# Inverse roots of eighteen norms: spread over the partitions through a line in DRAM instead of by matmuls

## The chip, the cores and the metric

The kernel runs on one core of a Trainium2 chip. The core has a matmul engine (PE, with its weight loads shown apart as PEld), three engines for elementwise work (DVE, ACT and POOL), a queue SP that issues most transfers, and 16 DMA engines. Each engine takes its own instructions in order and waits on semaphores for what others make. The metric is the device time of one execution in microseconds (us); lower is better.

## The reference

One decoder block on x of 2048 tokens with 1024 features, all in fp32:

```python
def rmsnorm(x, g):
    r = lax.rsqrt(jnp.mean(xf * xf, axis=-1, keepdims=True) + EPS)
    return xf * r * g

hn = rmsnorm(h, norm1_g)
proj = jnp.einsum('bsd,de->bse', hn, w_in)           # u_pool | q | k | v
y_pool = pool_mixer(u_pool, pool_w, pool_scale)
o = stick_breaking_attention(q, k, v)                 # 8 heads of 64
mixed = concatenate([rmsnorm(y_pool, pool_out_g), rmsnorm(o, attn_out_g)])
h = h + mixed @ w_out
hn2 = rmsnorm(h, norm2_g)
h = h + square(relu(hn2 @ w_up)) @ w_down             # 4096 wide
return rmsnorm(h, final_g)
```

Every `rmsnorm` needs, for each token, the inverse root `r` of the mean of the squares over its features.

## The kernel before

Activations lie transposed: features over the 128 partitions (P), tokens along the row. The 2048 tokens are four tiles j of T = 512 (NT = 4); 1024 features are KD = 8 chunks of 128. A tile of 512 tokens is TB = 4 blocks of 128.

A product in fp32 precision is made of three matmuls in fp32r: each operand is cut into a high and a low half by `split` (a copy on ACT, line 146, then a subtraction on DVE, line 147), and high by high, high by low and low by high are added (lines 178 to 180, 1102, 1275 and 1452). PE's stream is thus a long row of these matmuls: input projection, the attention of earlier tiles between them, output projection, and an FFN that takes two pairs of tiles and forms seven products in place of eight (`up` with PSUM tiles pX, pY, pZ; `down` with pb). Work beside the projections is put into a list `later` and let out a few pieces for each weight tile, so each engine's order is that in which the pieces are written, with the norms' root part set ahead by `tc.high_priority()`, and with `gates` that hold some work behind a marked matmul until PE's count of steps (`tick`) has passed.

A norm has these steps:

- `sum_squares` or its pieces: `ss` [128, 512] holds, for each partition, the sum of squares of the chunks.
- `mean_squares` (line 205): four matmuls of one column each, the 128 tokens of block c as stationary operand, `inv` (1/n) as moving one. The means of 512 tokens stand in `pm` as 128 partitions by 4 columns.
- `inv_root` (lines 213 to 224): one DVE operation that moves the means to `v`, then 13 small operations on POOL, a first guess by the bits and three Newton steps. The first norm of all does this on DVE.
- two POOL operations cut the root into halves `yr` (lines 241 and 242; 1320 and 1321 for the finals).
- `spread` (line 231): eight matmuls of 128x128 with a column of `yr`, repeated 128 times, as the stationary operand and an identity `identr` as the moving one. Then every partition of the PSUM tile `pr` holds the roots of all 512 tokens.
- ACT copies `pr` to `r` (line 251; 1327 for the finals; 1110 for `rlast`).
- DVE multiplies: `nt` = chunk x gain x `r` (line 263) and its like in norm2 (829), in the second FFN pair (960, with `rlast`) and in the final norm (1329). `split` of `nt` gives the tiles `h` or `mix` that PE reads.

19 norms go this way: norm1 of four tiles, the pool and attention norms of four tiles each, norm2 of two tiles by themselves and of two whose root is kept in `rlast` for the second FFN pair (`root_last`; its spreads stand inside `up`), and the final norm of three tiles (`final_root`, then `final_put` one step later). The last tile's final norm has steps of its own (`last_steps`) without a spread.

Of the kernel before, what the change touches and what calls it, by code (L numbers as in the profile page):

```python
# [46 lines left out]
def hymba_block(ctx: ExitStack, tc: tile.TileContext, xT, gains, w_in, pool_w, w_out, w_up, w_down, out):  # L47
# [74 lines left out]
    sslast = const.tile([P, T], F32, name="sslast")  # L122
    yrlast = const.tile([P, 2, 2, TB], F32R, name="yrlast")
    carry = const.tile([P, len(WINDOWS), PAD], F32, name="carry")
# [7 lines left out]
    mx = [[dram.tile([P, 2, T], F32R, name=f"mx{j}_{k}") for k in range(KD)] for j in range(NT)]  # L132
    hs = [dram.tile([KD, P, T], F32, name=f"hs{j}") for j in range(NT)]

    su = [[[dram.tile([P, 2, T], F32, name=f"su{q}_{i}_{c}") for c in range(2)] for i in range(7)] for q in range(2)]
# [63 lines left out]

    def mean_squares(parts, n, where=None, tag="px"):  # L200

        pm = (where or psx).tile([P, T], F32, tag=tag, name="pm")
        for c in range(TB):
            for i, ss in enumerate(parts):
                marks["pm"] = nc.tensor.matmul(pm[:, c:c + 1], ss[:, c * P:(c + 1) * P], inv[n],
                                               start=(i == 0), stop=(i == len(parts) - 1))
        return pm[:, 0:TB]
# [26 lines left out]

    def inv_rms(ss, n, r=None, eng=None, early=False):

        eng = eng or nc.gpsimd
        with tc.high_priority():
            y = inv_root(mean_squares([ss], n, psz if early else None, "pz" if early else "px"), eng)
            yr = tmp.tile([P, 2, TB], F32R, tag="yr", name="yr")  # L240
            eng.tensor_copy(yr[:, 0], y)
            eng.tensor_tensor(yr[:, 1], y, yr[:, 0].bitcast(F32), ALU.subtract)
            where, tag = (psx, "px") if eng is nc.vector else (psz, "pz") if early else (pst, "pt")
            pr = where.tile([P, T], F32, tag=tag, name="pr")
            marks["pr"] = spread(pr, yr)
            if eng is not nc.vector:
                g = state["tick"]
                gates.extend([(g + 10, marks["pm"]), (g + 14, marks["pr"])])
            if r is None:
                r = tmp.tile([P, T], F32, tag="r", name="r", bufs=2)  # L250
            nc.scalar.activation(r, pr, AF.Copy)
            return r

# [81 lines left out]
    def norm1_first():  # L335

        x, h = st[0]["x"], []
        for k in range(KD):
            d = make_h(0)
            a = nc.scalar.activation(d[:, 0], x[:, k], AF.Copy, scale=g1[:, k:k + 1])  # L340
            v = nc.vector.scalar_tensor_tensor(d[:, 1], x[:, k], g1[:, k:k + 1], d[:, 0].bitcast(F32),
                                               op0=ALU.mult, op1=ALU.subtract)
            h.append((d[:, 0], d[:, 1]))
        st[0]["h"] = h
        with tc.issue_after(a.ins), tc.issue_after(v.ins):
            ss = sum_squares([x[:, k] for k in range(KD)])
        st[0]["r"] = inv_rms(ss, D, root_tile(), nc.vector)

# [470 lines left out]
    def root_last(i, ss, where=None, tag="px"):  # L819
        y = inv_root(mean_squares([ss], D, where, tag), nc.gpsimd)  # L820
        nc.gpsimd.tensor_copy(yrlast[:, i, 0], y)
        nc.gpsimd.tensor_tensor(yrlast[:, i, 1], y, yrlast[:, i, 0].bitcast(F32), ALU.subtract)

# [37 lines left out]
    def up(pools, more):  # L861
# [221 lines left out]
        for g, (q, m, s) in enumerate(slots):  # L1083
# [21 lines left out]
            if g == 1:  # L1105
                root_last(1, sslast, psu, "R")
            elif g in (6, 10):
                pr, i = psu.tile([P, T], F32, tag="R", name="pr"), g // 10
                spread(pr, yrlast[:, i])
                nc.scalar.activation(rlast[:, i], pr, AF.Copy)  # L1110
            if g + UA < len(slots):
# [6 lines left out]
    def down(pools):  # L1118
# [197 lines left out]
        def final_root(j, acc, ss, r):  # L1316

            y = inv_root(mean_squares([ss], D, psb, f"b{free}"), nc.gpsimd)
            yr = tmp_.tile([P, 2, TB], F32R, tag="yr", name="yr", bufs=3)
            nc.gpsimd.tensor_copy(yr[:, 0], y)  # L1320
            nc.gpsimd.tensor_tensor(yr[:, 1], y, yr[:, 0].bitcast(F32), ALU.subtract)
            roots.append((j, acc, r, yr))

        def final_put(j, acc, r, yr):
            pr = psb.tile([P, T], F32, tag=f"b{free + 1}", name="pr")
            spread(pr, yr)
            nc.scalar.activation(r, pr, AF.Copy)
            for k in range(KD):
                nc.vector.scalar_tensor_tensor(acc[k], acc[k], gf[:, k:k + 1], r, op0=ALU.mult, op1=ALU.mult)
                nc.sync.dma_start(out[j, k], acc[k])  # L1330

        finals, roots, lastv = [], [], {}

# [104 lines left out]
        for g, (n_, i, kk, qs_) in enumerate(steps):  # L1438
# [26 lines left out]
            if n_ == "P3":  # L1465
                if qs_ == (1,):
                    free = 0
                if kk in (0, 2) and finals:
                    final_root(*finals.pop(0))
                elif kk in (1, 3) and roots:  # L1470
                    final_put(*roots.pop(0))
                elif kk == 4 and qs_ == (1,):
                    last_turn()
# [170 lines left out]
```

## Time and profile before

| | |
|---|---|
| median of 3 runs | 1904.19 us (1903.02 to 1910.56) |
| the profiled execution's span | 1902.6 us |
| PE busy | 1879.0 us, 99% |
| PEld, DVE, ACT busy | 82%, 78%, 54% |
| POOL busy | 179.5 us, 9% |
| DMA | 535.91 MB, mean 282 GB/s |
| mean granted PE clock | 0.996 |

The times are those of whole runs; the span goes from the first to the last instruction of one profiled execution, and the profile's rows lie in it. Busy time of PE comes from matmuls that overlap, so what a row of matmuls costs is read from the start of one group to the start of the next. Rows of the timeline give the start, the duration, engine and line, what is written and read, how many were put together, and in brackets the engine's idle time before it with what ended it.

### The profile page before, as it was taken

The page shows a single profiled execution, that of the slowest core. Times are in us where ns is not written, and L with a number is a line of the kernel's source. Part 1 is how long each engine was busy: PE and PEld are TensorE (multiplying, and loading weights), DVE is VectorE, ACT ScalarE, POOL GpSimd, SP SyncE. Part 2 cuts the span into 40 slices and gives each one's busy share as a digit, 9 for nine tenths or more (in the row PEclk, how much of TensorE's full clock was granted, in tenths as well). Part 3 has the DMA queues.
Part 4 walks back from the last instruction along what each step waited for, and adds up shares of the span by engine and source line. Part 5 has one row for each costly group of instructions (what it writes and reads, how often), then busy time and mean ns, then how long its engine had stood idle before and what let it go on. Part 6 is the DMA issues. An engine that isn't in the chain of part 4 may idle for free.

```text
span 1902.6 us, 26763 instructions
## 1 busy us (share of the span) xinstructions
PE 1879.0 (99%) x8947; PEld 1568.1 (82%) x8947; DVE 1481.2 (78%) x2216; ACT 1025.2 (54%) x1616; POOL 179.5 (9%) x399
## 2 busy tenths in 40 slices
PE   9999999999999999999999999999999999999997
PEld 7888888888888888888888888887888888888886
DVE  6887799667966886878799988786666677888774
ACT  5565576555654465454557555554432665656543
POOL 0211123101211030000000000000010010020120
PEclk9999999999999999999999999999999999999998
DMA  6686596788888777787899888889999799999852
GB/s 220 204 273 197 193 297 223 241 311 266 288 314 306 265 266 243 281 313 273 299 359 338 311 293 287 303 282 334 383 314 337 276 317 309 329 300 335 290 209 91
DMA packets 222164, 535.91 MB, mean 282 GB/s; under 512 B 26048, under 2 KB 32192, under 8 KB 218176
## 3 DMA queue, kind: packets, MB, share of 16 engines
q1 hardware_dynamic: 217264, 525.46, 79.3%
q0 software_dynamic: 4608, 8.39, 2.5%
q8 instruction: 72, 1.18, 0.2%
q14 instruction: 76, 0.62, 0.1%
q10 hardware_dynamic: 144, 0.26, 0.0%
HBM read 349.46 MB, written 184.55 MB: 281 GB/s over the span
## 4 chain that ended last, share of the span: by engine, by line
PE 49%; DMA 5%; DVE 3%; ACT 1%; issue 1%; POOL 0%; SPq 0%; DVEq 0%; ACTq 0%
PE pb L1275 13%; PE pY L1102 13%; PE pb L1452 12%; PE pZ L1102 7%; PE pX L1102 3%; DMA ar<-sd 2%; DMA ar<-sdi 1%; PE pb L1392 1%; DMA wr<-in_w_down_dram 0%; DMA b<-in_w_down_dram 0%; DMA t<-in_w_down_dram 0%; DMA td<-t 0%; DMA hn<-hs 0%; DVE hw L147 0%; DMA su<-hs 0%
## 5 line engine op out<-in xcount | busy, mean ns | idle before, releaser
L1102 PE MATMUL pY<-sa,hw 128*128 128x512 f32 x1536 | 366.2, 389 | 1.0 <-ACT u L1025 1.0
L1102 PEld LDWEIGHTS pY<-sa,hw 128*128 128x128 f32 x1536 | 288.0, 188 | 61.8 <-ACT u L1025 2.1
L1275 PE MATMUL pb<-ad,wd 128*128 128x512 f32 x1344 | 305.4, 389 | 0.7 <-DVE ad L147 0.7
L178 PE MATMUL pd<-h,hl 128*128 128x512 f32 x752 | 299.6, 398 | 0.7 <-DVE qkr L424 0.7
L180 PE MATMUL pd<-h,hl 128*128 128x512 f32 x752 | 296.8, 395 | 0.0
L1275 PEld LDWEIGHTS pb<-ad,wd 128*128 128x128 f32 x1344 | 252.1, 188 | 53.9 <-DVE ad L147 1.6
L179 PE MATMUL pd<-h,hl 128*128 128x512 f32 x752 | 296.5, 394 | 0.0
L1452 PE MATMUL pb<-ad,wd 128*128 128x512 f32 x1104 | 253.6, 390 | 1.3 <-ACT ad L146 1.2
L1452 PEld LDWEIGHTS pb<-ad,wd 128*128 128x128 f32 x1104 | 206.6, 188 | 44.7 <-ACT ad L146 1.7
L147 DVE TENSOR_TENSOR ad<-ar,ad 128x1024 fp32r<-128x1024 f32 x160 | 194.2, 1222 | 41.9 <-ACT ad L146 41.3
L146 ACT ACTIVATE ad<-ar 128x1024 fp32r<-128x1024 f32 x160 | 168.3, 1053 | 93.7 <-PE pb L1452 35.4
L1102 PE MATMUL pZ<-sa,hw 128*128 128x512 f32 x768 | 186.5, 389 | 0.8 <-DVE a L1045 0.8
L1102 PEld LDWEIGHTS pZ<-sa,hw 128*128 128x128 f32 x768 | 144.0, 188 | 31.1 <-DVE a L1045 1.2
L178 PEld LDWEIGHTS pd<-h,hl 128*128 128x128 f32 x752 | 142.1, 189 | 28.1 <-DVE qkr L424 1.0
L180 PEld LDWEIGHTS pd<-h,hl 128*128 128x128 f32 x752 | 141.8, 189 | 28.0
L179 PEld LDWEIGHTS pd<-h,hl 128*128 128x128 f32 x752 | 141.8, 189 | 26.9
L146 ACT ACTIVATE hl<-raw 128x512 fp32r<-128x512 f32 x168 | 103.8, 630 | 109.4 <-PE pd L180 70.5
L147 DVE TENSOR_TENSOR hl<-raw,hl 128x512 fp32r<-128x512 f32 x168 | 114.3, 686 | 53.2 <-ACT hl L146 50.1
L1019 ACT ACTIVATE a<-a 128x512 f32<-128x512 f32 x96 | 60.1, 629 | 88.5 <-DVE a L1061 38.1
L147 DVE TENSOR_TENSOR hw<-rt,hw 128x512 fp32r<-128x512 f32 x128 | 86.7, 687 | 24.1 <-ACT hw L146 24.0
L146 ACT ACTIVATE wd<-wq 128x1024 fp32r<-128x1024 f32 x56 | 59.4, 1061 | 79.4 <-PE pb L1275 69.0
L147 DVE TENSOR_TENSOR wd<-wq,wd 128x1024 fp32r<-128x1024 f32 x56 | 68.5, 1224 | 34.3 <-ACT wd L146 34.3
(220 smaller groups left out, 2719.1 us busy)
## 6 DMA issues: line engine op xcount, KB each, us to landing
ar<-sd SPq DMA_DIRECT2D x96, 512.0 KB, 5.9
ar<-sdi SPq DMA_DIRECT2D x64, 512.0 KB, 5.6
rb<-in_w_up_dram SPq DMA_DIRECT2D x30, 1024.0 KB, 6.6
sd<-a SPq DMA_DIRECT2D x104, 256.0 KB, 5.1
raw<-in_w_in_dram SPq DMA_DIRECT2D x50, 512.0 KB, 4.6
sdi<-hr SPq DMA_DIRECT2D x96, 256.0 KB, 5.2
wr<-in_w_down_dram SPq DMA_DIRECT2D x48, 512.0 KB, 5.6
sd<-s SPq DMA_DIRECT2D x88, 256.0 KB, 4.7
```

Source lines behind the costliest of these rows:

```text
L146: nc.scalar.activation(hi, src, AF.Copy)
L147: return nc.vector.tensor_tensor(lo, src, hi.bitcast(F32), ALU.subtract)
L178: nc.tensor.matmul(ps, hl[:, 0, c], hi, start=(k == 0), stop=False)
L179: nc.tensor.matmul(ps, hl[:, 0, c], lo, start=False, stop=False)
L180: mm = nc.tensor.matmul(ps, hl[:, 1, c], hi, start=False, stop=(k == n - 1))
L1019: nc.scalar.activation(t, src, AF.Relu)
L1102: nc.tensor.matmul(t, w[:, wx, c], a[:, ax, c % 2], start=first and c == 0 and x == 0, stop=last and c == G - 1 and x == 2, skip_group_che ...
L1275: nc.tensor.matmul(b, t[:, wx, 2 * (kk % 2) + c, i * P:(i + 1) * P], a[:, ax, c], start=p in ("P1", "P5", "P2") and kk == 0 and c == 0 and ...
L1392: nc.tensor.matmul(b[:, cols], block(t, wx, c, n), a[:, ax, c, cols], start=False, stop=(i == 1 and c == 1 and x == 2), skip_group_check=True)
L1452: nc.tensor.matmul(ps[q, n], block(t, wx, c, n), left_[q][:, ax, c], start=(n_ in ("P1", "P3") and kk == 0 and c == 0 and x == 0), stop=(n ...
```

## The change

For all norms but the first and the last tile's final one, the root is no longer cut into halves and spread by PE. A new `to_all` writes the root from POOL's DMA queue (128 partitions by 4 fp32) as a line of 512 numbers, 2 KB, into DRAM, and SP's queue reads that line back into all 128 partitions of `r`. There is one line for each norm.

So that the line stands in the order of the tokens, `mean_squares` now takes every fourth token for a column (token 4p + c in partition p, column c) instead of a block of 128 tokens that lie side by side. The first norm keeps blocks, DVE's root and the spread. The matmuls of `spread`, the `yr` halves, the PSUM tiles `pr` and ACT's copies go; `up` loses its two spreads after steps 6 and 10; `final_put` only multiplies; `gap` tiles hold the place of what went in the on-chip memory. The gate on the mean's matmul stays, that on `pr` goes.

```diff
@@ -120,7 +120,7 @@
     zeros = const.tile([1, 1], I32, name="zeros")
     rlast = const.tile([P, 2, T], F32, name="rlast")
     sslast = const.tile([P, T], F32, name="sslast")
-    yrlast = const.tile([P, 2, 2, TB], F32R, name="yrlast")
+    const.tile([P, 4 * TB], F32, name="gap")
     carry = const.tile([P, len(WINDOWS), PAD], F32, name="carry")
     nc.vector.memset(carry, 0.0)
 
@@ -131,6 +131,7 @@
     os_ = [dram.tile([H // 2, P, T], F32, name=f"os{j}") for j in range(NT)]
     mx = [[dram.tile([P, 2, T], F32R, name=f"mx{j}_{k}") for k in range(KD)] for j in range(NT)]
     hs = [dram.tile([KD, P, T], F32, name=f"hs{j}") for j in range(NT)]
+    roots = [dram.tile([1, T], F32, name=f"root{i}") for i in range(32)]
 
     su = [[[dram.tile([P, 2, T], F32, name=f"su{q}_{i}_{c}") for c in range(2)] for i in range(7)] for q in range(2)]
     sd = [[[dram.tile([P, 2, T], F32, name=f"sd{q}_{i}_{c}") for c in range(8)] for i in range(7)] for q in range(2)]
@@ -197,13 +198,12 @@
             add_square(ss, c, i == 0)
         return ss
 
-    def mean_squares(parts, n, where=None, tag="px"):
+    def mean_squares(ss, n, where=None, tag="px", blocks=False):
 
         pm = (where or psx).tile([P, T], F32, tag=tag, name="pm")
+        by = ss.rearrange("p (c t) -> p c t", c=TB) if blocks else ss.rearrange("p (t c) -> p c t", c=TB)
         for c in range(TB):
-            for i, ss in enumerate(parts):
-                marks["pm"] = nc.tensor.matmul(pm[:, c:c + 1], ss[:, c * P:(c + 1) * P], inv[n],
-                                               start=(i == 0), stop=(i == len(parts) - 1))
+            marks["pm"] = nc.tensor.matmul(pm[:, c:c + 1], by[:, c], inv[n], start=True, stop=True)
         return pm[:, 0:TB]
 
     def inv_root(pm, eng):
@@ -232,24 +232,33 @@
                                       start=(b == 0 and x == 0), stop=(b == TB - 1 and x == 1), skip_group_check=True)
         return mm
 
-    def inv_rms(ss, n, r=None, eng=None, early=False):
-
-        eng = eng or nc.gpsimd
+    roots_out = []
+
+    def to_all(r, y):
+
+        line = roots[len(roots_out)]
+        roots_out.append(line)
+        nc.gpsimd.dma_start(line.rearrange("o (p c) -> (o p) c", c=TB), y)
+        nc.sync.dma_start(r, line.to_broadcast([P, T]))
+        return r
+
+    def inv_rms(ss, n, r=None, first=False, early=False):
+
         with tc.high_priority():
-            y = inv_root(mean_squares([ss], n, psz if early else None, "pz" if early else "px"), eng)
-            yr = tmp.tile([P, 2, TB], F32R, tag="yr", name="yr")
-            eng.tensor_copy(yr[:, 0], y)
-            eng.tensor_tensor(yr[:, 1], y, yr[:, 0].bitcast(F32), ALU.subtract)
-            where, tag = (psx, "px") if eng is nc.vector else (psz, "pz") if early else (pst, "pt")
-            pr = where.tile([P, T], F32, tag=tag, name="pr")
-            marks["pr"] = spread(pr, yr)
-            if eng is not nc.vector:
-                g = state["tick"]
-                gates.extend([(g + 10, marks["pm"]), (g + 14, marks["pr"])])
+            if first:
+                y = inv_root(mean_squares(ss, n, blocks=True), nc.vector)
+                yr = tmp.tile([P, 2, TB], F32R, tag="yr", name="yr")
+                nc.vector.tensor_copy(yr[:, 0], y)
+                nc.vector.tensor_tensor(yr[:, 1], y, yr[:, 0].bitcast(F32), ALU.subtract)
+                pr = psx.tile([P, T], F32, tag="px", name="pr")
+                marks["pr"] = spread(pr, yr)
+                nc.scalar.activation(r, pr, AF.Copy)
+                return r
+            y = inv_root(mean_squares(ss, n, psz if early else None, "pz" if early else "px"), nc.gpsimd)
+            gates.append((state["tick"] + 10, marks["pm"]))
             if r is None:
                 r = tmp.tile([P, T], F32, tag="r", name="r", bufs=2)
-            nc.scalar.activation(r, pr, AF.Copy)
-            return r
+            return to_all(r, y)
 
     def rms(chunks):
         return inv_rms(sum_squares(chunks), len(chunks) * P)
@@ -344,7 +353,7 @@
         st[0]["h"] = h
         with tc.issue_after(a.ins), tc.issue_after(v.ins):
             ss = sum_squares([x[:, k] for k in range(KD)])
-        st[0]["r"] = inv_rms(ss, D, root_tile(), nc.vector)
+        st[0]["r"] = inv_rms(ss, D, root_tile(), first=True)
 
     def norm1_rms(j):
         def square(k):
@@ -817,9 +826,7 @@
         return took
 
     def root_last(i, ss, where=None, tag="px"):
-        y = inv_root(mean_squares([ss], D, where, tag), nc.gpsimd)
-        nc.gpsimd.tensor_copy(yrlast[:, i, 0], y)
-        nc.gpsimd.tensor_tensor(yrlast[:, i, 1], y, yrlast[:, i, 0].bitcast(F32), ALU.subtract)
+        to_all(rlast[:, i], inv_root(mean_squares(ss, D, where, tag), nc.gpsimd))
 
     def norm2(j):
         acc = [st[j]["acc"][:, k] for k in range(KD)]
@@ -1104,10 +1111,6 @@
             post(q, m, s)
             if g == 1:
                 root_last(1, sslast, psu, "R")
-            elif g in (6, 10):
-                pr, i = psu.tile([P, T], F32, tag="R", name="pr"), g // 10
-                spread(pr, yrlast[:, i])
-                nc.scalar.activation(rlast[:, i], pr, AF.Copy)
             if g + UA < len(slots):
                 make_weights(g + UA)
                 q2, m2, s2 = slots[g + UA]
@@ -1315,21 +1318,16 @@
 
         def final_root(j, acc, ss, r):
 
-            y = inv_root(mean_squares([ss], D, psb, f"b{free}"), nc.gpsimd)
-            yr = tmp_.tile([P, 2, TB], F32R, tag="yr", name="yr", bufs=3)
-            nc.gpsimd.tensor_copy(yr[:, 0], y)
-            nc.gpsimd.tensor_tensor(yr[:, 1], y, yr[:, 0].bitcast(F32), ALU.subtract)
-            roots.append((j, acc, r, yr))
-
-        def final_put(j, acc, r, yr):
-            pr = psb.tile([P, T], F32, tag=f"b{free + 1}", name="pr")
-            spread(pr, yr)
-            nc.scalar.activation(r, pr, AF.Copy)
+            tmp_.tile([P, 2, TB], F32, tag="gap", name="gap", bufs=3)
+            to_all(r, inv_root(mean_squares(ss, D, psb, f"b{free}"), nc.gpsimd))
+            ready.append((j, acc, r))
+
+        def final_put(j, acc, r):
             for k in range(KD):
                 nc.vector.scalar_tensor_tensor(acc[k], acc[k], gf[:, k:k + 1], r, op0=ALU.mult, op1=ALU.mult)
                 nc.sync.dma_start(out[j, k], acc[k])
 
-        finals, roots, lastv = [], [], {}
+        finals, ready, lastv = [], [], {}
 
         def bank(b):
             return psb.tile([P, T], F32, tag=f"b{b}", name=f"pb")
@@ -1467,8 +1465,8 @@
                     free = 0
                 if kk in (0, 2) and finals:
                     final_root(*finals.pop(0))
-                elif kk in (1, 3) and roots:
-                    final_put(*roots.pop(0))
+                elif kk in (1, 3) and ready:
+                    final_put(*ready.pop(0))
                 elif kk == 4 and qs_ == (1,):
                     last_turn()
         last_steps(held, PAIRS[1][0])
```

On SP, at the first tile's pool norm (`raw` are weights of the projection, `qa`, `qb`, `kw` and `vw` operands of the attention's matmuls), before:

```order
L429 DMA ks_0_201<-qk 64x512
L160 DMA raw<-in_w_in_dram 128x1024
L704 DMA vw<-vs_0_221 128x512
L610 DMA qa<-qs_0_165 128x512
L611 DMA qb<-qs_0_165 64x512
L612 DMA qb<-qs_0_165 64x512
L703 DMA kw<-ks_0_197 128x512
```

and now:

```order
L438 DMA ks_0_201<-qk 64x512
L161 DMA raw<-in_w_in_dram 128x1024
L242 DMA r<-root_286 128x512
L713 DMA vw<-vs_0_221 128x512
L619 DMA qa<-qs_0_165 128x512
L620 DMA qb<-qs_0_165 64x512
L621 DMA qb<-qs_0_165 64x512
L712 DMA kw<-ks_0_197 128x512
```

The read of `r` stands between `raw` and `vw`; it waits for POOL's write, and what follows waits behind it. At the second tile's norm1 the read stands in the same way right behind `raw`, ahead of `qa`.

On DVE, at the same pool norm (`pc`, `sg`, `at` and `ot` belong to the attention, `vf` to the projection, `yb` is the pool mixer's output), before, behind the mean's move to `v`:

```order
L635 TENSOR_TENSOR ot<-ot,po 64x512
L147 TENSOR_TENSOR at<-pta,at 128x384
L147 TENSOR_TENSOR at<-pta,at 128x512
L629 SCALAR_TENSOR_TENSOR pc<-sh 128x128
L629 SCALAR_TENSOR_TENSOR pc<-sh 128x256
L436 TENSOR_TENSOR vf<-pd,r_624 128x512
...
L655 TENSOR_TENSOR sg<-sg,pc 128x127
L655 TENSOR_TENSOR sg<-sg,pc 128x255
L263 SCALAR_TENSOR_TENSOR nt<-yb,gains,r 128x512 x3
L147 TENSOR_TENSOR at<-pta,at 128x384
```

and now:

```order
L148 TENSOR_TENSOR hl<-raw,hl 128x512
L644 TENSOR_TENSOR ot<-ot,po 64x512
L148 TENSOR_TENSOR at<-pta,at 128x384
L272 SCALAR_TENSOR_TENSOR nt<-yb,gains,r 128x512
L148 TENSOR_TENSOR at<-pta,at 128x512
L272 SCALAR_TENSOR_TENSOR nt<-yb,gains,r 128x512 x2
L638 SCALAR_TENSOR_TENSOR pc<-sh 128x128
L638 SCALAR_TENSOR_TENSOR pc<-sh 128x256
L445 TENSOR_TENSOR vf<-pd,r_656 128x512
L638 SCALAR_TENSOR_TENSOR pc<-sh 128x256 x2
L148 TENSOR_TENSOR mix<-nt,mix 128x512
L148 TENSOR_TENSOR qk<-pd,qk 128x512
```

The first products with `r` moved forward: one stands between the two splits of `at`, and two more ahead of the next scans. At the second tile's norm1 DVE's rows are the same as before.

On PE, in `up` of the first FFN pair, where one of the roots for `rlast` is made, before:

```order
L205 MATMUL pm<-inv_115,sslast 128x1 x4
L1102 MATMUL pZ<-sa,hw 128x512 x8
L1102 MATMUL pY<-sa,hw 128x512 x24
L231 MATMUL pr<-identr,yrlast 128x128 x8
L1102 MATMUL pX<-sa,hw 128x512 x2
L1102 MATMUL pY<-sa,hw 128x512 x12
L1102 MATMUL pX<-sa,hw 128x512 x10
L1102 MATMUL pY<-sa,hw 128x512 x24
L1102 MATMUL pZ<-sa,hw 128x512 x24
L231 MATMUL pr<-identr,yrlast 128x128 x8
```

and now:

```order
L206 MATMUL pm<-inv_115,sslast 128x1 x4
L1109 MATMUL pZ<-sa,hw 128x512 x8
L1109 MATMUL pY<-sa,hw 128x512 x24
L1109 MATMUL pX<-sa,hw 128x512 x2
L1109 MATMUL pY<-sa,hw 128x512 x12
L1109 MATMUL pX<-sa,hw 128x512 x10
L1109 MATMUL pY<-sa,hw 128x512 x24
L1109 MATMUL pZ<-sa,hw 128x512 x24
```

Both groups of eight spread matmuls are gone and the products stand against each other.

## The prediction

> **What bounds the kernel now.** I read the head of the page, the chain, the view of the tile `pr` (which the spread writes), then the timeline at single norms, the DMA issues and the stretches.
>
> ```profile
> span 1902.6 us, 26763 instructions
> PE 1879.0 (99%) x8947; PEld 1568.1 (82%) x8947; DVE 1481.2 (78%) x2216; ACT 1025.2 (54%) x1616; POOL 179.5 (9%) x399
> PE 49%; DMA 5%; DVE 3%; ACT 1%; issue 1%; POOL 0%; SPq 0%; DVEq 0%; ACTq 0%
> ```
>
> PE is busy for 99% of the span, and is the largest part of the chain that ended last. So a matmul taken away is worth its own time on PE, and a wait newly put on PE costs its own length. VectorE (DVE) has 22% free, but it feeds PE in order.
>
> ```profile
> L231 PE MATMUL pr<-identr,yr x136: 221/274/415, 37.3 to 1860.2; 128*128 128x128 f32 x136
> L231 PE MATMUL pr<-identr,yrlast x16: 221/274/277, 709.2 to 727.1; 128*128 128x128 f32 x16
>   POOL yr L241: 2.9, 1
>   POOL yr L1320: 2.2, 2
>   DVE nt L263: 6.4, 5
>   DVE c L1329: 2.1, 1
> ```
>
> These are 152 spread matmuls, eight for each of 19 norms; the first norm keeps its eight, so 144 go. The two POOL lines say that the weight loads of a spread sat idle until POOL had the root; the last two say that DVE already waited for the finished `r` in a few norms.
>
> **The gain.** Eight spread matmuls in PE's stream:
>
> ```profile
> 709.19 1.00 PE L231 MATMUL pr<-identr,yrlast 128*128 128x128 f32 x8
> 710.03 0.67 PE L1102 MATMUL pX<-sa,hw 128*128 128x512 f32 x2
> ```
>
> Durations overlap, so the price is from start to next start: 710.03 − 709.19 = 0.84 us. 18 × 0.84 = 15.1 us off PE, with nothing else of PE's in that time. The waits for the root go too, where the spread stood at the head of PE's queue:
>
> ```profile
> 455.45 0.39 PE L179 MATMUL pd<-h,hl 128*128 128x512 f32 x1
> 458.36 0.33 PE L231 MATMUL pr<-identr,yr 128*128 128x128 f32 x1 [2.52 <-DVE pc L629]
> 1807.09 0.33 PE L231 MATMUL pr<-identr,yr 128*128 128x128 f32 x1 [0.87 <-POOL yr L1320]
> 458.00:461.00 3.00, 2.65 (x14) 2.54 (x15) 1.47 (x3) 1.02 (x2) 1.09 (x3) 0.70 1.05 380
> 461.00:464.00 3.00, 3.00 (x11) 2.36 (x11) 2.35 (x5) 0.81 (x2) 0.00 (x0) 0.73 0.86 277
> 464.00:467.00 3.00, 3.00 (x20) 2.65 (x19) 0.57 (x1) 1.05 (x3) 0.00 (x0) 1.00 0.57 158
> ```
>
> 2.5 + 0.9 = 3.4 us of waiting. The three stretches show PEclk, the third number from the end: after the stop of 2.5 us the granted clock is 0.70 and 0.73 for 6 us, then 1.00 again. That is 6 × (1 − 0.715) = 1.7 us more, and the price of any new stop of that length. Gain: 15.1 + 3.4 + 1.7 = 20.2 us.
>
> **What costs nothing.** 18 of the 19 copies of `pr` on ACT (0.6 us each, as the row of such a copy below shows) leave an engine that is 54% busy; the first norm's stays. POOL loses 36 small operations and gains 18 DMA issues; POOL is 9% busy, and what stands behind an issue there (15-column copies, `left`) has slack while the issue is about 1 us; uncovered it would cost under 1 us a norm. The freed PSUM banks change no wait that I can find.
>
> **The new stationary.** The mean now loads its weights from every fourth column of `ss`, and the view of `pm` and the timeline know only columns side by side:
>
> ```profile
> L205 PEld LDWEIGHTS pm<-inv,ss x144: 187/192/192, 28.5 to 1850.8; 128*128 128x128 f32 x144
> 58.66 1.09 PEld L205 LDWEIGHTS pm<-inv,ss 128*128 128x128 f32 x8
> ```
>
> Eight loads follow each other at (1.09 − 0.19) / 7 = 0.13 us. If the stride does nothing, 0; if it halves the rate, 144 × 0.13 = 18.7 us. I take 0, as every load in the rows, of whatever tile, has the same 0.19 us, and keep 18.7 for the range. The Trainium skill, "SBUF — State Buffer" (Specifications), says that SBUF wants at least two hits on each 16-byte line, and four fp32 are just such a line; by it the load would be slower and the sum up to 18.7 us higher. No run of before shows a strided load. This rule is the second half of the slow rival below.
>
> **The new path of `r`.** From the finished root to `r` in all partitions there are now a 2 KB write from POOL's queue, and, once it has landed, a 256 KB read on SP's queue.
>
> ```profile
> L1250 POOL DMA_DIRECT2D u<-hs x16: 862/1170/1758, 1682.1 to 1722.1; - x16
> u<-hs POOLq DMA_DIRECT2D x16, 256.0 KB, 8.9
> qa<-qs SPq DMA_DIRECT2D x32, 256.0 KB, 4.5
> su<-hn SPq DMA_DIRECT2D x16, 256.0 KB, 2.6
> qs<-qk SPq DMA_DIRECT2D x64, 128.0 KB, 3.4
> ```
>
> The last number is from issue to landing. Low end: two of the fastest 256 KB transfers, 2.6 + 2.6 = 5.2 us. High end: POOL's accumulating 256 KB and the attention's loads, 8.9 + 4.5 = 13.4. The write is small, so I put it at the smallest transfer in the rows (3.4) plus POOL's own issue (1.2), 4.6; the read has the size of both SP rows, 3.4 lies between them. I take 8.0 us. The Trainium skill, "DMA: Bandwidth & Descriptors" (Anatomy of one DMA — SWDGE), gives about 2 us of fixed cost to a transfer; by it both together would take about 4 to 5 us, below my low end, and the change would be the fast rival. The rows, with nothing under 2.6 us in the median, are above it, though none is that small.
>
> How long did it take before? The root is ready where POOL's cast starts, `r` where ACT's copy ends:
>
> ```profile
> 68.58 0.19 POOL L241 CAST yr<-v 128x4 fp32r<-128x4 f32 x1
> 71.10 0.60 ACT L251 ACTIVATE r<-pr 128x512 f32<-128x512 f32 x1 [1.74 <-PE pr L231]
> 1856.86 0.19 POOL L1320 CAST yr<-v 128x4 fp32r<-128x4 f32 x1
> 1860.47 0.60 ACT L1327 ACTIVATE rf<-pr 128x512 f32<-128x512 f32 x1 [1.09 <-PE pr L231]
> ```
>
> These are the first and the last of the pairs: 3.1 and 4.2 us; over the 13 norms whose consumer stands right behind `r` the mean is 4.3. So `r` comes 8.0 − 4.3 = 3.7 us later on average, and DVE, which meets its consumer in order, stands still with all that is queued behind it: splits of weights, evacuations of PSUM, the attention's scans.
>
> The second tile's norm1:
>
> ```profile
> 71.78 2.07 DVE L263 SCALAR_TENSOR_TENSOR nt<-xt,gains,r 128x512 f32<-128x512 f32 x3
> 74.38 1.29 DVE L147 TENSOR_TENSOR h<-nt,h 128x512 fp32r<-128x512 f32 x2
> 76.19 0.40 PE L178 MATMUL pd<-h,hl 128*128 128x512 f32 x1
> ```
>
> `nt` moves from 71.78 to 68.58 + 8.0 = 76.6, by 4.8 us. The first of the two splits of `h` ended at about 75.1 (half of 1.29 after 74.38), PE read it at 76.19: 1.1 us of slack. PE stops for 3.7 us, and 1.7 for the clock: 5.4.
>
> The first tile's pool norm, whose consumer the order puts further forward:
>
> ```profile
> 102.92 0.53 POOL L241 CAST yr<-v 128x4 fp32r<-128x4 f32 x1
> 105.94 1.31 DVE L147 TENSOR_TENSOR at<-pta,at 128x384 fp32r<-128x384 f32 x2
> 107.99 0.76 PE L675 MATMUL po<-at,vw 128*128 128x256 f32 x5
> 114.41 2.07 DVE L263 SCALAR_TENSOR_TENSOR nt<-yb,gains,r 128x512 f32<-128x512 f32 x3
> ```
>
> Before, `nt` came at 114.41, long after both `at`. Now one `nt` stands between the two `at`: r at 102.92 + 8.0 = 110.9, `nt` 0.7, `at` 0.7, so 112.3, where PE read it at 107.99. PE stops for 4.3, and 1.7: 6.0 us.
>
> Nine more norms of tiles' first half have a consumer that DVE meets soon: 9 × 3.7 = 33 us of DVE standing still. Nothing of it reaches PE at one end (no row above shows PE stopping behind DVE's 6.4 us), all 33 at the other.
>
> ```profile
> 150.00:250.00 100.00, 98.90 (x528) 83.56 (x527) 77.51 (x131) 56.10 (x104) 16.99 (x46) 1.00 0.65 214
> 350.00:450.00 100.00, 100.00 (x560) 85.98 (x559) 66.59 (x109) 52.17 (x95) 7.88 (x27) 1.00 0.88 293
> ```
>
> Behind PE's and PEld's stands DVE's busy time of 100 us: 78 and 67, so DVE has room to catch up, while PE has none. I take a third, 11 us, nearer to the row that cost nothing. The finals: 3 × 3.7 = 11 of DVE's time; DVE's 2.1 us wait for `rf` before stopped no matmul of the main stream, so 0 (at the other end 11). The two roots that the second half of FFN pairs use (`rlast`) are read over 50 us after, and the two `ra` over 4: 0.
>
> **The sum.** −20.2 + 5.4 + 6.0 + 11 = +2.2 us: span 1902.6 → 1904.8. The median of the runs, 1904.2, lies 1.6 above this profile's span, so 1906.4; I write 1906.
>
> **The rivals.** *Fast: the lateness is hidden.* With 5.2 us, `r` is late by 0.9 on average; the tile's norm1 loses 2.1 − 1.1 = 1.0, the pool norm 109.5 − 107.99 = 1.5, both too short for the clock, the nine a third of 8, 2.7: −20.2 + 5.2 = −15, 1889. If all is hidden, 1884. For it: PE lost little to DVE's waits so far. Against it: a chain of two transfers where the fastest group has 2.6. It decides below about 6 us for both.
>
> *Slow: `r` later, or SP's queue held.* With 10 us, norm1 loses 5.7 + 1.7, the pool norm 6.3 + 1.7, the nine half of 9 × 5.7, 26: +21, 1925; with the strided loads at 18.7 as well, 1944. Its other place is SP: the read of `r` waits there until the write has landed, and what is queued behind it waits too.
>
> ```profile
> 102.43 0.53 SPq L160 DMA_DIRECT2D raw<-in_w_in_dram  x1
> 104.70 0.33 SPq L704 DMA_DIRECT2D vw<-vs  x1
> 106.39 0.32 SPq L610 DMA_DIRECT2D qa<-qs  x1
> ```
>
> At the pool norm the read stands between `raw` and `vw`: SP would be held until 102.92 + 4.6 = 107.5, and `vw` goes out 2.8 us late. Where such a load has less lead than that, PE stops for it. It decides where both take over 9.5 us, or where more than half of the nine's lateness reaches PE.
>
> *The change doesn't do what it says* is excluded: the order shows 144 spread matmuls fewer.
>
> **How the numbers follow.** About 0.5%, 9.5 us, is what a measurement of this kernel tells from no change, so faster is under 1894.7 and slower over 1913.7. My case (7 to 9 us, 1896 to 1918) 0.44: of it 0.02 faster, 0.28 same, 0.14 slower. Fast (1884 to 1896) 0.32: 0.30 faster, 0.02 same. Slow (1914 to 1944) 0.24. In all 0.32, 0.30, 0.38. The range of 8 in 10 runs from inside the fast case to the middle of the slow one, 1887 to 1930; my case alone 1896 to 1918.
>
> **What would show it.** PE's instructions 144 fewer, its busy time about 15 lower; issue to landing of the writes near 4.6 and of the reads near 3.4; DVE's `nt` with an idle time until the DMA `r` of some 4 us in each norm; PE stops of about 4 us at the second tile's norm1 and the first pool norm, with a clock near 0.7 behind them; no stop at 455 and 1806; L205's loads still 0.19 us. I am wrong if both transfers take under 6 us or over 10, if PE stops for loads of the attention, or if the loads of `ss` get longer.

## The result, and the profile after

| | before | changed |
|---|---|---|
| median | 1904.19 us | 1976.54 us |
| runs | 1903.02 to 1910.56 | 1972.71 to 1978.54 |
| span of the profiled execution | 1902.6 us | 1970.7 us |

The changed kernel is slower, by a ratio of 1.038 (95% interval 1.0363 to 1.0397). Forecast were 1906 us and at most 1930. The head of the changed kernel's page:

```profile
span 1970.7 us, 26483 instructions
PE 1905.1 (97%) x8803; PEld 1584.2 (80%) x8803; DVE 1479.7 (75%) x2216; ACT 1016.8 (52%) x1598; POOL 188.3 (10%) x381
PE 70%; DMA 12%; DVE 10%; issue 3%; POOL 3%; ACT 2%; SPq 1%; DVEq 0%; ACTq 0%; POOLq 0%
```

PE has 144 matmuls fewer, as the change says, and is yet busy for 26.1 us more (1905.1 − 1879.0); its idle time went from 23.6 to 65.6 us. In the chain that ended last, DMA has 12% instead of 5, and the roots' transfers are part of it now. So the 68.1 us of span are 42.0 of stops and 26.1 of slower work, and the slower work has to be taken apart.

First the spreads: 18 x 0.84 = 15.1 us are gone. Then the loads of the means. The view of `pm` after, and the eight loads of `sslast` in PE's timeline, which took 0.80 us from start to next start before (700.99 to 701.79):

```profile
L206 PEld LDWEIGHTS pm<-inv,ss x144: 187/329/332, 27.1 to 1919.6; 128*128 128x128 f32 x144
763.05 1.80 PE L206 MATMUL pm<-inv,sslast 128*128 128x1 f32 x8
764.71 1.63 PE L1109 MATMUL pZ<-sa,hw 128*128 128x512 f32 x6
```

A load with a step of four columns takes 329 ns (median) instead of 192, and eight matmuls of a mean 764.71 − 763.05 = 1.66 us: 0.86 more, 18 x 0.86 = 15.5 us. That eats the whole of what the spreads gave. The rest of PE's slower work is 26.1 + 15.1 − 15.5 = 25.7 us. The clock accounts for it: the mean granted clock fell from 0.996 to 0.982, which over the two spans makes 0.018 x 1970.7 − 0.004 x 1902.6 = 28 us (an estimate, from rounded means).

Why PE stops is in the waits of PE, here the longest groups (waiting line, what ended the wait, us in all, times, longest):

```profile
PE pd L179 <- DVE acc L823: 15.4, 3, 7.6
PE po L684 <- DVE at L148: 8.9, 5, 5.2
PE pb L1450 <- DVE wd L148: 4.4, 1, 4.4
PE pta L673 <- DVE sg L668: 4.0, 3, 2.4
PE pd L179 <- DVE qk L148: 3.8, 1, 3.8
PE pp L406 <- ACT pls L147: 3.7, 1, 3.7
```

None of these names a root. PE waits for evacuations of PSUM, splits and attention pieces that DVE and ACT make in the ordinary way. In the timelines, stops of 27 us in all come within some 15 us behind a wait of DVE for a root (PE is back at 77, 78, 118, 272 to 278, 314, 393, 680 and 1906 us): what PE reads there stands behind the products with `r` in DVE's order. The other stops come behind something else, as the longest group shows: of its 15.4 us, 2.9 follow a wait for `r` (at 680), 7.6 come from SP (the second case below), and 5.0 come at 633, behind the eight products of norm2 in one row, for which DVE did not wait:

```profile
624.05 5.38 DVE L836 SCALAR_TENSOR_TENSOR acc<-acc,gains,r 128x512 f32<-128x512 f32 x8
632.77 0.77 PE L179 MATMUL pd<-h,hl 128*128 128x512 f32 x1 [4.95 <-DVE acc L823]
```

DVE's waits, from the whole list of waits, and SP's:

```profile
DVE nt L272 <- DMA r<-root: 35.3, 9, 5.6
DVE c L1327 <- DMA rf<-root: 16.9, 2, 10.4
SPq L242 <- DMA root<-v: 81.6, 16, 19.7
```

With two groups of 3.5 and 3.4 us more (`acc` of norm2, `p` of the finals), DVE stood still for 59.1 us until a read of a root had landed. SP stood still for 81.6 us ahead of such a read, until the write of its line had landed. Three cases follow. The first tile's pool norm:

```profile
110.23 0.54 DVE L148 TENSOR_TENSOR at<-pta,at 128x384 fp32r<-128x384 f32 x1
116.36 0.75 DVE L272 SCALAR_TENSOR_TENSOR nt<-yb,gains,r 128x512 f32<-128x512 f32 x1 [5.58 <-DMA r<-root]
117.03 0.68 DVE L148 TENSOR_TENSOR at<-pta,at 128x512 fp32r<-128x512 f32 x1
117.76 1.33 PE L684 MATMUL po<-at,vw 128*128 128x256 f32 x5 [5.24 <-DVE at L148]
```

DVE waits 5.58 us for `r`, the second `at` behind it is late, and PE waits 5.24 us for that. It is the stop that the prediction priced at 4.3. What the clock does at this stop, in stretches of 3 us (PEclk is third from the end):

```profile
112.00:115.00 3.00, 0.52 (x5) 0.29 (x3) 0.00 (x0) 0.57 (x2) 0.00 (x0) 1.00 0.29 80
115.00:118.00 3.00, 0.24 (x1) 0.24 (x2) 1.65 (x3) 0.86 (x2) 0.00 (x0) 0.67 1.01 283
118.00:121.00 3.00, 2.71 (x12) 2.32 (x13) 3.00 (x6) 2.35 (x5) 0.00 (x0) 0.50 0.56 124
121.00:124.00 3.00, 3.00 (x13) 2.50 (x12) 3.00 (x7) 0.87 (x2) 0.57 (x1) 0.70 0.90 284
```

Of the 6 us behind the stop, PE works 3 at 0.50 and 3 at 0.70: 1.5 + 0.9 = 2.4 us more, near half of the stop again.

The second case is the first root for `rlast`, on SP, ACT and DVE:

```profile
723.62 0.32 SPq L824 DMA_DIRECT2D hs<-acc  x1
734.37 0.32 SPq L242 DMA_DIRECT2D rlast<-root  x1
734.79 0.86 SPq L946 DMA_DIRECT2D sr<-su  x2
741.11 1.06 ACT L147 ACTIVATE sa<-sr 128x1024 fp32r<-128x1024 f32 x1 [11.96 <-DMA sr<-su]
742.20 1.23 DVE L148 TENSOR_TENSOR sa<-sr,sa 128x1024 fp32r<-128x1024 f32 x1 [11.60 <-ACT sa L147]
```

SP issues nothing from 723.9 to 734.4, since its next instruction waits until the root has been made and written. The load `sr` behind it comes late, ACT and DVE stand still for some 12 us at its split, and PE for 7.6 at `acc` (the longest wait in PE's list). Nobody needs `rlast` here.

The third case is a final norm, for which the forecast had nothing:

```profile
1899.01 2.74 DVE L1327 SCALAR_TENSOR_TENSOR c<-c,gains,rf 128x512 f32<-128x512 f32 x4 [10.45 <-DMA rf<-root]
1901.66 2.74 DVE L1327 SCALAR_TENSOR_TENSOR u<-u,gains,rf 128x512 f32<-128x512 f32 x4
1905.59 0.80 PE L1450 MATMUL pb<-ad,wd 128*128 128x512 f32 x1 [4.39 <-DVE wd L148]
1908.00:1911.00 3.00, 3.00 (x9) 2.35 (x8) 3.00 (x5) 1.46 (x3) 0.00 (x0) 0.50 0.97 356
```

DVE waits 10.45 us for `rf`, then multiplies for 5.4 us, and the split of the next weights `wd` stands behind that: PE stops for 4.39 us, with half of its clock after it.

### The profile page after: what moved, and what is told of

The parts are those of the page before. It is cut to its first block, busy times and chain, and to the rows that moved or that the text cites. A ratio compares the mean times of both kernels' runs of the same rounds, so it can differ in the third digit from the quotient of the medians.

```text
span 1970.7 us, 26483 instructions
## 1 busy us (share of the span) xinstructions
PE 1905.1 (97%) x8803; PEld 1584.2 (80%) x8803; DVE 1479.7 (75%) x2216; ACT 1016.8 (52%) x1598; POOL 188.3 (10%) x381
## 4 chain that ended last, share of the span: by engine, by line
PE 70%; DMA 12%; DVE 10%; issue 3%; POOL 3%; ACT 2%; SPq 1%; DVEq 0%; ACTq 0%; POOLq 0%
PE pb L1278 15%; PE pY L1109 12%; PE pb L1450 10%; PE pZ L1109 6%; PE pd L179 5%; PE pd L180 5%; PE pd L181 5%; PE pX L1109 3%; DMA t<-in_w_down_dram 2%; DMA root<-v 2%; DMA r<-root 1%; PE pm L206 1%; PE po L684 1%; DVE nt L272 1%; DVE hw L148 1%
## 5 line engine op out<-in xcount | busy, mean ns | idle before, releaser
L179 PE MATMUL pd<-h,hl 128*128 128x512 f32 x752 | 305.8, 407 | 22.2 <-DVE acc L823 15.4
L180 PE MATMUL pd<-h,hl 128*128 128x512 f32 x752 | 302.0, 402 | 1.4 <-DVE h L148 1.4
L181 PE MATMUL pd<-h,hl 128*128 128x512 f32 x752 | 301.5, 401 | 1.9 <-DVE hl L148 1.9
L179 PEld LDWEIGHTS pd<-h,hl 128*128 128x128 f32 x752 | 145.8, 194 | 53.4 <-ACT sq L189 8.0
L181 PEld LDWEIGHTS pd<-h,hl 128*128 128x128 f32 x752 | 145.2, 193 | 32.7 <-DVE hl L148 3.1
L180 PEld LDWEIGHTS pd<-h,hl 128*128 128x128 f32 x752 | 145.8, 194 | 29.7 <-DVE h L148 1.7
```

Source lines behind the costliest of these rows:

```text
L179: nc.tensor.matmul(ps, hl[:, 0, c], hi, start=(k == 0), stop=False)
L180: nc.tensor.matmul(ps, hl[:, 0, c], lo, start=False, stop=False)
L181: mm = nc.tensor.matmul(ps, hl[:, 1, c], hi, start=False, stop=(k == n - 1))
```

## The experiments

Two theories stood against each other. The first: *the root's way through DRAM is too long for the place where DVE meets `r`*. The second: *SP, held until the write has landed, sends other loads late*. Beside them stood the stride, the order of the engines and the transfers' own traffic. The ratios are to the kernel before, and the edits are shortened, with `...` for what is left out.

**The stride alone, in the kernel before.**

```diff
-  matmul(pm[:, c:c + 1], ss[:, c * P:(c + 1) * P], inv[n], ...)
+  matmul(pm[:, c:c + 1], ss.rearrange("p (t c) -> p c t", c=TB)[:, c], inv[n], ...)   # but the first norm
```

> The kernel before, with one thing of the change: the means of the 18 norms load every fourth column of the sums of squares (the spread is kept; the roots then stand at other tokens than they belong to, which leaves the values wrong and the work the same). All engines keep the order of before. In the changed kernel these loads follow each other at 0.233 us in place of 0.112. Theory 'stride costs PE': 18 x 8 x 0.121 = 17.4 us more, 1921 to 1924. Rival 'the loads are hidden or a stall takes them up': within 4 us of 1904.

1921.3 us against 1905.2 beside it, ratio 1.008 (1.0063 to 1.0096): 16 us more, as the theory that the stride costs PE had it (1921 to 1924). All engines keep their order, so this is the stride alone. The loads are 329 ns there too:

```profile
L205 PEld LDWEIGHTS pm<-inv,ss x144: 188/329/332, 29.8 to 1867.3; 128*128 128x128 f32 x144
```

**The changed kernel without the stride.**

```diff
-  by = ss.rearrange("p (c t) -> p c t", c=TB) if blocks else ss.rearrange("p (t c) -> p c t", c=TB)
+  by = ss.rearrange("p (c t) -> p c t", c=TB)
```

> The changed kernel with columns side by side for every norm (the line in DRAM then has the roots at other tokens, values wrong, work the same). All engines keep the order of the changed kernel. Theory 'stride costs PE, beside the waits': 17 us less, 1957 to 1962. Rival 'PE waits anyway, the loads only fill its waits': less than 6 us off 1976.

1964.4 us, ratio 1.0306 (1.0287 to 1.0325): 12 us less than the changed kernel, with its order on every engine. That lies between the two forecasts, 17 us and under 6, and the five runs spread from 1961.2 to 1978.3. The stride is a cost beside the waits; whether some of it fills waits that PE has anyway is not shown.

**The read on POOL's queue.**

```diff
-  nc.sync.dma_start(r, line.to_broadcast([P, T]))
+  nc.gpsimd.dma_start(r, line.to_broadcast([P, T]))
```

> The changed kernel with the read of r issued from POOL's queue behind its own write, not from SP's. Theory 'SP is held': SP waited 81.6 us for the writes with loads of weights and of the FFN's sums behind; freed of it, the stop of 7.8 us at 736 and those about 620 go, and with their clock the time falls by 15 to 30 us, to 1946 to 1962, though r itself is no earlier. Rival 'DVE meets r late, SP is no matter': no gain, and as POOL's transfers of 256 KB took 8.9 us in the kernel before against 4.2 for SP's read now, r is later and the time 1976 to 2010.

1971.1 us, ratio 1.0343 (1.0319 to 1.0366), 5 us less. The result lies between the two forecasts: the stop at 736 is gone, but DVE's wait for roots grew, from 59.1 to 63.3 us. At the first tile's pool norm, on POOL and DVE:

```profile
110.44 0.59 POOL L241 DMA_DIRECT2D root<-v  x1 [0.29 <-POOL v L224]
115.36 0.56 POOL L242 DMA_DIRECT2D r<-root  x1 [4.03 <-DMA root<-v]
121.77 2.08 DVE L272 SCALAR_TENSOR_TENSOR nt<-yb,gains,r 128x512 f32<-128x512 f32 x3 [7.23 <-DMA r<-root]
```

What SP's freedom gave, `r` took back by coming later: 11.3 us from the write's issue to `nt`, against 8.9 in the changed kernel.

**The read of a line that is ready.**

```diff
-  nc.sync.dma_start(r, line.to_broadcast([P, T]))
+  nc.sync.dma_start(r, roots[-1].to_broadcast([P, T]))     # filled with ones at the start
```

> The changed kernel with the write of each root as it is, but the read of r from a line that was written at the start of the kernel, so neither SP nor DVE waits for the root (values wrong, work the same; the order of the engines is another, since r is ready sooner). Theory 'all that is lost beside the stride is waiting for the root's way through DRAM': 1904 - 15 (spreads) - 5 (their waits and clock) + 17 (stride) = 1901, range 1896 to 1908. Rival 'the order without the spreads, or the transfers' traffic, is itself worse': above 1920.

1912.6 us, ratio 1.0035 (1.0019 to 1.0051): 64 us less than the changed kernel. All writes, all reads and the stride are still there, so these do not cost the 64 us; what is gone is the waiting for the root, on SP and on DVE, and with it the order of the engines that went with the waiting. It came out 12 us over the forecast's middle, and the start holds about half of that: PE's first 60 matmuls end 5.5 us later than in the kernel before, with a wait of 3.7 us for `h` that the changed kernel does not have. That the reads of the ready line, which now stand among the first loads of x, are the cause is not shown.

**Only the two reads of `rlast` on POOL's queue.**

```diff
-  to_all(rlast[:, i], inv_root(...))
+  to_all(rlast[:, i], inv_root(...), nc.gpsimd)      # the read's queue
```

> The changed kernel with only the two reads of rlast issued from POOL's queue, all else as it is and PE's order the same. SP waited 10.4 and 9.4 us at these two reads, with the FFN's sums sr and weights behind, though rlast itself is read over 50 us after. Theory 'SP held is a cost of its own': the stop of 7.8 us at 736 goes, with some 2 us of clock: 8 to 11 us less, 1965 to 1969. Rival 'the stop comes of something else (the missing spreads let PE run ahead of the loads)': within 3 us of 1976.

1964.0 us, ratio 1.0315 (1.0296 to 1.0334): 12.5 us less, a little over the theory's 8 to 11, and no stop about 736. PE's order is the same row by row (DVE's and ACT's differ in a few rows), so this is the price of SP's hold at a place where no one waits for the root: for the two reads together a stop and its clock.

**Two Newton steps.**

```diff
-  for _ in range(3):
+  for _ in range(3 if eng is nc.vector else 2):
```

> The changed kernel with two Newton steps on POOL in place of three (values a little off): each root is ready 4 POOL operations sooner, some 1.1 to 2.4 us, and the way through DRAM is as it was. Theory 'the time goes by how late r is': E4 took away some 8 us of lateness for 64 us, so 8 us per us of lateness: 9 to 19 us less, 1957 to 1968. Rival 'the transfers themselves, their traffic or the order, cost the time': under 4 us less.

1956.4 us, ratio 1.0273 (1.0255 to 1.0291): 20 us less for roots that are one step sooner, with the same transfers; the theory had 9 to 19. DVE's waits for roots fell by less than half of that, from 59.1 to 49.6 us, so the time goes with how late `r` is, but not one for one. Part of it may be the order, which differs in places.

**A ready line and no stride.** The edits of the fourth and the second together.

> The read of a line that is ready from the start, and the columns of ss side by side: the order is that of e4. Theory 'terms add': 1912.6 - 16 = 1896 to 1898, below the kernel before, by the spreads that are gone. Rival 'without the loads' 17 us PE meets its other waits sooner': 1902 to 1908.

1900.7 us, ratio 0.998 (0.9965 to 0.9995): 12 us under the fourth experiment, as the second was under the changed kernel. All engines keep the order of the fourth, so this is once more the stride alone. The result lies between the forecasts. PE is busy for 1867.3 us, 11.7 less than before, so most of the spreads' 15.1 us is there; but its first 60 matmuls end 7.0 us later than before, so only 3.7 us of time are won. With a start as before, a free way of the roots would bring some 11 us (an estimate, 3.7 + 7.0).

**Only the roots of `rlast` through DRAM, in the kernel before,** written in 512 pieces of 4 bytes.

```diff
-  nc.gpsimd.tensor_copy(yrlast[:, i, 0], y)  ...  spread(pr, yrlast[:, i])
+  nc.gpsimd.dma_start(lines[i].rearrange("o (c p) -> (o p) c", c=TB), y)
+  nc.gpsimd.dma_start(rlast[:, i], lines[i].to_broadcast([P, T]))
```

> The kernel before (spreads, columns side by side) with only the two roots for rlast through DRAM, written and read from POOL's queue in the order of the tokens. Nobody reads rlast for 50 us and POOL has little to do there, so nothing should wait: two groups of spread matmuls go, 2 x 0.84 = 1.7 us less, 1902 to 1904, at the edge of what can be told. Rival 'POOL held or transfers in the way': 1906 to 1912.

1908.3 us, ratio 1.0017 (1.0006 to 1.0028): in the rival's range, and no gain even where 50 us lie between root and reader. The trace holds a stop of PE that the kernel before does not have, and shows what stands ahead of it. The first of the two writes was issued at 673.90 and took some 11 us; meanwhile the 16 DMA engines moved little:

```profile
678.00:682.00 4.00, 4.00 (x20) 3.30 (x19) 3.13 (x4) 1.24 (x2) 0.00 (x0) 1.00 1.27 62
682.00:686.00 4.00, 3.75 (x17) 2.78 (x15) 0.00 (x0) 0.00 (x0) 0.47 (x1) 1.00 0.57 81
689.24 0.77 PE L178 MATMUL pd<-h,hl 128*128 128x512 f32 x1 [3.49 <-ACT sa L146]
```

The last number of the first two rows is GB/s: 62 and 81, where the kernel before has 343 and 297 in the same stretches. A load of weights issued beside the write, at 674.74, took 11.7 us to land, where the median of its line is 4.9. PE stops for 3.49 us behind these loads. So the write in small pieces went together with a delay of transfers that have nothing to do with it. One trace shows this; the order of DVE and SP, which differs from before at many places, may have its part in the 4 us.

**Nobody waits for `r`.**

```diff
-  nc.vector.scalar_tensor_tensor(t, chunk_of(i), g[:, i:i + 1], r(), ...)
+  nc.vector.scalar_tensor_tensor(t, chunk_of(i), g[:, i:i + 1], sslast, ...)     # set to 1 at the start; norm2 and finals alike
```

> The changed kernel with a constant tile in place of r, ra and rf in DVE's products (values wrong, work the same; writes, reads and SP's waits for them stay, rlast too). It splits the 64 us of e4 into DVE's meeting r late and SP's being held. Theory 'DVE's wait is the most of it, SP's hold the 12 us of e5 and a little more': 1913 + 12 + up to 8 = 1925 to 1933. Rival 'SP's hold is the most': 1945 to 1965. The order differs from the changed kernel's as in e4.

1917.7 us, ratio 1.0067 (1.0047 to 1.0086), under the range of the first theory. SP is still held, as its list of waits says:

```profile
SPq L242 <- DMA root<-v: 84.3, 15, 17.2
```

84.3 us of SP's waiting cost at most 5.1 us over the fourth experiment (1917.7 − 1912.6). So of the 64 us, 59 are gone when DVE no longer waits for `r`. Two things keep this from being the price of DVE's wait alone. The 12.5 us of `rlast` are not seen here, with another order of SP, so they are among the 59: what a hold costs depends on the loads that stand behind it. Without them it is 46. And DVE's order is another one, here and in the fourth experiment: the eight products of norm2, which stand in one row in the changed kernel, stand in groups of two and three with evacuations between them. No run took away DVE's wait and kept the order, so the 46 to 59 us are the price of both together.

**Products two pieces later.** On the kernel of the fifth experiment.

```diff
-  later.extend(lambda i=i: chunk(i) for i in range(n))
+  later.extend([lambda: None] * 2 + [lambda i=i: chunk(i) for i in range(n)])     # norm2 alike
```

> e5 (1964 us) with the products of norm1, pool, attention and norm2 let out of the list two pieces later, so that DVE has other work while r is on its way. Theory 'DVE meets r too early in its order': its waits for r fall and with them 10 to 30 us, 1934 to 1954. Rival 'PE needs what the products make at that time anyway': the stop only moves, 1960 to 1972.

1948.6 us, ratio 1.023 (1.0212 to 1.0248): 15.5 us less than the fifth experiment, inside the first theory's range. DVE's `nt` still waits, 28.4 us instead of 33.0, the finals as before. All its waits for roots fell by no more than 3.7 us (from 57.7 to 54.0), so most of the gain is in where the waits fall and not in their length. A later place helps, but two pieces are not enough.

**Two Newton steps in the kernel before.** The edit of the sixth.

> The kernel before (spreads, no DRAM) with two Newton steps on POOL in place of three. PE waited for the root 2.5 + 0.9 us before two spreads, and ran at 0.70 to 0.73 of its clock for 6 us behind the first. With the root 1.1 to 2.4 us sooner, theory 'PE's waits for the root and their clock are all that is left of it': 2 to 5 us less, 1899 to 1902. Rival 'hidden, or the order shifts': within 2 us of 1904.

1912.4 us, ratio 1.0049 (1.0032 to 1.0066): slower. PE's two waits for roots became one of 0.9 us and a new one of 2.0 before a spread of `rlast`, and other waits came up. Both forecasts missed. Sooner roots go with another order of the engines; that this order is what costs the 9 us is a guess that no run tested.

**All remedies at once,** with the line written in the order of the tokens, so that columns may lie side by side:

```diff
-  nc.gpsimd.dma_start(line.rearrange("o (p c) -> (o p) c", c=TB), y)
+  nc.gpsimd.dma_start(line.rearrange("o (c p) -> (o p) c", c=TB), y)
```

> The changed kernel with every single remedy at once: reads of rlast from POOL's queue, products two pieces later (both e10, 1948.6), columns side by side (-12 to -16 by e2 and e1) with the line written in the order of the tokens, in 512 pieces of 4 bytes, and two Newton steps (-20 by e6, of which later products have taken some). Theory 'the terms add for the most part': 1915 to 1930, still slower than before. Rival 'the write in pieces makes r later, and takes back what the others give': 1932 to 1950.

2030.6 us, ratio 1.0664 (1.0647 to 1.0682), beyond even the rival. The write's issue to landing (min, median, max, us), in the changed kernel and here, and DVE's waits here:

```profile
DMA to landing us min/median/max: 1.7/3.3/8.6
```

```profile
DMA to landing us min/median/max: 8.5/10.0/15.0
DVE nt L272 <- DMA r<-root: 74.9, 9, 12.7
DVE c L1327 <- DMA rf<-root: 29.4, 2, 17.5
```

In 512 pieces of 4 bytes the write takes 6.7 us longer (median) than in 128 of 16. With `p` and `acc` (15.5 and 12.5) DVE waits 132.3 us, where the kernel of the tenth experiment had 54.0 (28.4 + 17.0 + 4.7 + 3.9). The time rose by 82.1 us for 78.3 of waiting, although the stride and a Newton step were gone. How much of it is the late `r`, and how much comes of other transfers beside the pieces, as in the eighth experiment, these runs do not tell apart.

## Why the prediction was wrong, point by point

- *The gain of 15.1 us from the spreads*: right in kind and nearly in size. PE's matmuls are fewer by 144, and with the stride and the waits taken away (experiment 7) PE is busy for 11.7 us less.
- *The way of `r`, 8.0 us*: right in sum. The writes take 3.3 us (median) where 4.6 were forecast, the reads 4.2 where 3.4 were; that the two errors nearly cancel is luck. At the second tile's norm1, from POOL's issue to `nt`, it is 7.2 us:

```profile
67.87 0.74 POOL L241 DMA_DIRECT2D root<-v  x1 [0.32 <-POOL v L224]
71.10 0.33 SPq L242 DMA_DIRECT2D r<-root  x1
75.10 1.42 DVE L272 SCALAR_TENSOR_TENSOR nt<-xt,gains,r 128x512 f32<-128x512 f32 x2 [3.81 <-DMA r<-root]
```

  At the pool norm it is 8.9. Of the rows, the SP ones between 2.6 and 4.5 were the right guide. The 2 us of the Trainium skill, "DMA: Bandwidth & Descriptors" (Anatomy of one DMA — SWDGE), held only for the shortest write, 1.7.
- *DVE's lateness, 3.7 us in each of 13 norms, 48 us*: 59.1 us of waiting against some 9 before, right in size.
- *A third of it reaches PE in nine norms, and nothing of the finals*: this is the step that failed. With the two norms worked out by themselves, the sum had 5.4 + 6.0 + 11 + 0 = 22.4 us for `r` coming late. The trace shows 27 us of stops behind DVE's waits for roots, near half of the 59.1, among them 4.4 at a final norm; the clock comes on top. Experiments 5 and 9 put the whole at 46 to 59 us, with the change of order in it. The row that the third leaned on, DVE's 6.4 us of waiting before without a stop, came from five waits of at most 2.2 us. That the slack behind them took these up, and does not take up 4 to 6 us, fits the rows; no run varied the slack alone.
- *The clock, 1.7 us at two places*: too few. PE lost 25.7 us more beside the stops, where the forecast had 3.4. The price of one stop was of the right size (2.4 at the pool norm), the number of stops was not.
- *The stride, taken as 0*: failed too, 16 us in experiment 1 and 12 in experiments 2 and 7. The forecast reasoned that every load in the rows took 0.19 us; but no row had a stride, and that was no evidence. Its bound of 18.7 for half the rate was near. The Trainium skill, "SBUF — State Buffer" (Specifications), asks for two hits on a 16-byte line for full bandwidth; the 329 ns against 192 agree with that, and no run tried a smaller step.
- *`rlast` at 0*: failed as well. The prediction asked when its reader comes, not what SP has behind the read: 12.5 us in experiment 5. It named SP's hold in the slow rival, at the pool norm; there PE's stop ended with the late `at` and not with a load.
- *The slow rival* had 1925, and 1944 with the stride, at 10 us of way and half of the lateness. What came was 8 us of way, near half of the lateness as stops, the clock on top of them, the stride and SP's hold.
- *What is left*: the time is 70 us over the forecast. The lateness (24 to 37 more than forecast), the stride (12 to 16) and `rlast` (12.5, if not already in the 37) make some 50, so about 20 us stand in no term. Three groups of stops that the prediction has no term for may be most of them, 3.7 us at 224, 2.8 between 600 and 617 and 5.0 at 633, with the clock on top; their cause stays open.

## What to carry to other kernels

Where an engine in order meets a late operand, count all that is queued behind it as late too, and compare the lateness with the slack of the first thing behind that the bottleneck reads. What is over the slack is a stop, and a share taken from shorter waits says nothing about longer ones: here it was near half in place of a third, and 25.7 us of clock came on 42.0 us of stops. A transfer that waits in a shared queue costs by what is queued behind it, not by when its own result is read. And an operand read with a step where it lay side by side is to be priced as unknown, even for eight small loads, when no row shows a step.

## What the runs showed of the hardware

A stationary operand read at a step of 16 bytes loads in 329 ns instead of 192. At the stop of 5.2 us the clock fell while PE stood still (mean 0.67 from 115 to 118, with PE back at 117.76), and in stretches of 1 us it was 0.50 up to 122 and 1.00 from 123 on, some 5 us after PE was back. Behind a stop of 2.5 us the mean over 3 us was 0.70. The Trainium skill, "TensorE: Matmul & The Clock Gate" (Part 1: The HAM clock gate), names two states, full and half rate, and the 0.50 here agrees. The values between are means of stretches in which the clock changed: the 0.70 of 121 to 124 is made of 0.50, 0.59 and 1.00.

A write of 2 KB from 128 partitions took 1.7 to 8.6 us, and in pieces of 4 bytes 8.5 to 15.0. Beside one such write in pieces, all transfers together moved 62 to 81 GB/s for 8 us, where the kernel before moved 297 to 343.
